# Smaller first transfers, bias copies one at a time, and weight blocks moved by 64 or 192 bytes

## The chip, the cores and the metric

One core of a Trainium2 chip runs the whole kernel as a single program. The metric is device time in microseconds (us), the median of repeated runs. A profile of one execution is shown beside it; "span" is the time from its first to its last instruction.

## The reference, cut to what matters

Two transformer blocks run one after the other on x of 512 rows by 1024 columns, all in float32. The first has a mixing layer of two kinds of attention, then cross attention to a memory of 256 rows, then an MLP; the second has windowed attention, a gated unit and another MLP.

```python
h = rms_norm(x, norm_mix[l])
proj = h @ w_in[l]
qa, ka, va, qg, kg, vg, glr, rg = jnp.split(proj, offsets, axis=-1)
o_a = moba_attention(qa, ka, va, rp_table)      # scores + a bias by distance, softmax, values
o_g = gla_chunked(qg, kg, vg, log_a)            # gated linear attention
x = x + concat(o_a, norm(o_g) * silu(rg)) @ w_out[l]
...                                             # cross attention, MLP, then the second block
```

The bias of a score depends on the head and on the distance between query and key alone.

## The kernel before

**Products.** All large matrix products are made of float32r matmuls of 128 rows by 128 weight columns by up to 512 moving columns. Each operand is split into a high part and a low part, so one product is three matmuls (`mm3`: high by high, high by low, low by high). `ah` and `al` hold the two parts of the normed activations, transposed, as 8 slices of 512 columns.

**Weights.** `weight_order` lists all weight units in the order of use. `load` (line 219) takes one unit: it allocates a block for the high part and one for the low part (`whi`, `wlo`, or one block `wu` for both where a unit has 1024 columns) from 10 slots of the tag `u8`, and then for each piece issues a DMA on SyncE's queue (SP) into one of three staging tiles `st` (line 233), an ACT copy that rounds to the high part (line 234) and a DVE subtraction for the low part (line 235). A unit of `w_in_u` is two pieces of 512 KB. `weight` (line 240) asks for the next unit and loads one unit ahead.

**Which operand is the weight block.** In `fm` the weight block is the stationary operand and `ah`/`al` move; in `tm` the activations are stationary and the weight block moves. Products with 256 moving columns are: `tm256` on units 2, 4, 7 and 9 of `w_in_u` (96 matmuls each), `mem_kv` on `w_xk` and `w_xv` (four units of 48 each), `fm_halves` on the first two units of `w_xq` and on units 2 and 3 of `w_in_2f` (96 each), `heads_v` on the two units of `w_in_2v` (96 each), and the first four units of `w_up` and of `w_up_2` (48 each). That is 384 + 384 + 384 + 192 + 384 = 1728 matmuls of the kernel's 8930 recorded ones. The first two units, `w_in_a`, are moved with 264 columns, so their slices of one k lie 1056 bytes apart.

**Places in SBUF.** A slot of `u8` has the size of its largest tile, 8 times 264 words, which is 8448 bytes or 33 times 256. In the built kernel `ah`, `al`, every `u8` block and the tiles of the phase pools start 192 bytes above a multiple of 256. `ident`, the moving operand of the transposes, starts 64 bytes lower in that count (128 above a multiple of 256): the tiles between it and `ah` are 512, 64, 512 and 2048 bytes, which is 12 times 256 and 64 more.

**Start.** `block1_mix` (line 404) loads the transposed x in four parts of two k slices (`x_piece`) between the three pieces of `w_in_a` unit 0 (rows k 0 to 2, 3 to 5, 6 to 7); only the first part comes in two transfers. Then the rows of x (`xin`) are loaded for the row sums.

**Bias of the attention scores.** `rel_bias` (line 540) makes a table `gd` of 8 heads by 640 distances in DRAM. `skew` (line 559) copies two heads of it to a DRAM tile `rd`, once for each of 128 rows (639 KB), so that a read with a shifted row length (`wbias`, line 569) gives the bias of two heads with the diagonal in place. There are four such copies: `rel_bias` calls `skew` once and each of the four `moba` calls calls it once more behind its own `wbias` load, until four are made. They depend on `gd` alone.

**Order.** The order of work is traced through small generator threads with hand-set delays; a planner of the framework then orders the instructions of each queue by that trace and by its own estimate of when each can start. Every engine and SP then works through its list in order: an instruction that waits holds up all that stand behind it on its engine. In the stretch that matters here the main thread runs, for each of two pairs: `pair` (line 514) for the linear attention's q and k, `pair` for the first attention pair's q and k, `moba` on these, `tm256` for v, another `pair` and `moba`, and `tm256` again.

Of the kernel before, what the change touches and what calls it, by code (L numbers as in the profile page):

```python
# [10 lines left out]
F32R = mybir.dt.float32r  # L11
# [9 lines left out]
P = 128  # L21
# [9 lines left out]
N_K2 = 19  # L31
N_M8 = 6
SCRATCH = 1024

PAD = 48
AHEAD = 1
# [6 lines left out]
def f32(ap):  # L43
    return ap.bitcast(F32)
# [65 lines left out]
class Kernel:  # L110
# [100 lines left out]
    def weight_ahead(self, n):  # L211
        while self.order and len(self.loaded) < n:
# [3 lines left out]
            else:  # L216
                self.loaded.append((o[:2], self.load(*o)))

    def load(self, key, idx, nk, w, after=None):

        nc = self.nc
        if nk * w == 1024:
            hl = self.u8([P, 2, nk, w], F32R, "wu")
            hi, lo = hl[:, 0], hl[:, 1]
        else:
            hi = self.u8([P, nk, w], F32R, "whi")
            lo = self.u8([P, nk, w], F32R, "wlo")
        src = self.I[key][idx].rearrange("p (a b) -> p a b", a=nk)
        step = 1024 // w
        for a in range(0, nk, step):  # L230
            s = slice(a, min(a + step, nk))
            st = self.sb.tile([P, s.stop - a, w], F32, tag="st", bufs=N_ST, name=self.name("st"))
            nc.sync.dma_start(st, src[:, s, :])
            nc.scalar.activation(hi[:, s, :], st, AF.Copy)  # L234
            nc.vector.tensor_sub(lo[:, s, :], st, f32(hi[:, s, :]))  # L235
            if after:
                after(a // step)
        return hi, lo

    def weight(self, *key, ahead=AHEAD):  # L240
# [163 lines left out]
    def block1_mix(self):  # L404
        nc, I, th = self.nc, self.I, self.th
        self.t_aux, self.t_tr = Tokens(2), Tokens(2)

        gm = self.sm([P, KT], "gmix")
        ex = [Event() for _ in range(KT)]

        def x_piece(j):
            st = self.k4([P, 2, T], F32, "xT")
            src = I["x_T"][j].rearrange("p (a t) -> p a t", a=2)
            if j:
                nc.sync.dma_start(st, src)
            for i in range(2):
                k = 2 * j + i
                if j == 0:
                    nc.sync.dma_start(st[:, i, :], src[:, i, :])
                if k == 0:  # L420
                    nc.sync.dma_start(gm, I["norm_mix"])
                if k == 1:
                    self.loaded.append((o[:2], self.load(*o, after=after)))
                nc.scalar.activation(self.ah[:, k, :], st[:, i, :], AF.Copy, scale=gm[:, k : k + 1])
                nc.vector.scalar_tensor_tensor(self.al[:, k, :], st[:, i, :], gm[:, k : k + 1], f32(self.ah[:, k, :]),
                                               op0=ALU.mult, op1=ALU.subtract)
                th.fire(ex[k])

        def after(i):
            if i < 2:  # L430
                x_piece(i + 1)
                if i == 1:
                    x_piece(3)

        o = self.order.pop(0)
        x_piece(0)
        self.weight_ahead(2)
        nc.sync.dma_start(self.ident, I["c_ident"])
        ss = self.sm([P, NC], "ssx")
        for c in range(NC):  # L440
            t = self.k4([P, D], F32, "xin")
            nc.sync.dma_start(t, I["x"][self.cs(c), :])
            nc.scalar.activation(self.junk, t, AF.Square, accum_out=ss[:, c : c + 1])
        rs = self.rstd(ss, NC, D)
        rsb = self.k2([P, T], F32, "rsb")

        va = self.u8([P, NC, 512], F32, "va")
        glr = self.k2([P, NC, 16], F32, "glr")
        w = self.weight("w_in_a", 0)
        ps = [self.acc() for _ in range(NC)]  # L450
        for k in range(KT):
            yield ex[k]
            for c in range(NC):
                self.mm3(ps[c][:, :264], *self.a_chunk(c)(k), w[0][:, k, :], w[1][:, k, :], k == 0, k == KT - 1)
        for c in range(NC):
            nc.scalar.activation(glr[:, c, :], ps[c][:, :16], AF.Copy, scale=rs[:, c : c + 1])
            nc.scalar.activation(va[:, c, 0:248], ps[c][:, 16:264], AF.Copy, scale=rs[:, c : c + 1])
        w = self.weight("w_in_a", 1)
        for c in range(NC):
            ps = (self.aux if c < 2 else self.tr)()  # L460
            self.tm(ps[:, :264], self.a_chunk(c), [w])
            nc.scalar.activation(va[:, c, 248:512], ps[:, :264], AF.Copy, scale=rs[:, c : c + 1])
        self.spread(rsb, rs, NC)
        self.rs, self.rsb = rs, rsb
        self.rel_bias()
        self.gla_consts(glr)
        yield 0.4
        oa = self.u8([P, NC, 512], F32, "oa")
        og = self.u8([P, 2, NC, 2, P], F32, "og")
        em = self.mem_norm()  # L470
        eo, eg = [Event() for _ in range(4)], [Event() for _ in range(2)]

        u = 0
        for pr in range(2):
            q, k, ev = yield from self.pair(u, 0.125)
            evr, vr = Event(), []
            th.spawn(self.gla(pr, q, k, ev, vr, evr, og[:, pr], eg[pr]), 2)
            q, k, ev = yield from self.pair(u + 1, -0.125)
            th.spawn(self.moba(2 * pr, q, k, ev, va, oa, eo[2 * pr]), 3)
            vr.append(self.k4([P, NC, 256], F32, "vg"))  # L480
            yield from self.tm256(u + 2, AF.Copy, vr[0])
            q, k, ev = yield from self.pair(u + 3, -0.125)
            th.spawn(self.moba(2 * pr + 1, q, k, ev, va, oa, eo[2 * pr + 1]), 3)
            vr.append(self.k4([P, NC, 256], F32, "rg"))
            yield from self.tm256(u + 4, AF.Silu, vr[1])
            th.fire(evr, 0.53)
            u += 5
        win = Event()
        th.fire(win)
        mix = [Event() for _ in range(NC)]  # L490

        def mix_T(c):
            yield eo + eg + [win]
            hi, lo = self.ah[:, :, self.cs(c)], self.al[:, :, self.cs(c)]
            self.split(oa[:, :, self.cs(c)], hi[:, 0:4, :], lo[:, 0:4, :])
            self.to_T(lambda k: og[:, k // 2, c, k % 2, :], 4, hi[:, 4:, :], lo[:, 4:, :])
            th.fire(mix[c], 2.29)

        for c in range(NC):
            th.spawn(mix_T(c), 1)  # L500
        yield from self.mem_kv(em)
        self.mix = mix
# [8 lines left out]
            self.mm(ps[:, self.cs(c)], self.ones, d, True, True)  # L511
        nc.scalar.activation(out, ps[:, : n * P], AF.Copy)

    def pair(self, u, sc):

        w = self.weight("w_in_u", u)
        ts = []
        for m in range(2):
            ps = self.acc()
            self.fm(ps, w, m, self.a_all())  # L520
            t = self.k2([P, T], F32, "qk")
            self.nc.vector.scalar_tensor_tensor(t, ps, sc if m == 0 else 1.0, self.rsb, op0=ALU.mult, op1=ALU.mult)
            ts.append(t)
            yield
        ev = Event()
        self.th.fire(ev, 1.12)
        return *ts, ev
# [31 lines left out]
    def skew(self):  # L559

        pr = len(self.rd)
        if pr < 4:
            self.rd.append(self.dp.tile([2, P * 639], F32, name=f"rd{pr}"))
            self.nc.sync.dma_start(self.rd[pr].rearrange("h (p l) -> p h l", l=639),
                                   self.gd[None, 2 * pr : 2 * pr + 2, :639].to_broadcast([P, 2, 639]))

    def moba(self, pr, q, k, ev, va, oa, done):
        nc, th = self.nc, self.th
        bias = self.k4([P, 2, 512], F32, "wbias")
        nc.sync.dma_start(  # L570
            bias, self.rd[pr][:, 127 : 127 + P * 638].rearrange("h (p l) -> p h l", l=638)[:, :, :512])
        self.skew()

        qd, ks = ([self.k2([P, T], F32R, n) for _ in range(2)] for n in ("qd", "ks"))
        ql = self.k2([P, T], F32R, "ql")
        for hh in range(2):
            o, x = slice(64 * hh, 64 * hh + 64), slice(64 - 64 * hh, 128 - 64 * hh)
# [1044 lines left out]
```

## Time and profile before

| | us |
|---|---|
| median of 3 runs | 1622.96 |
| lowest and highest of them | 1621.26, 1623.02 |
| time of the profiled execution | 1621.62 |
| span of its profile | 1619.8 |

The profile names engines PE (matmul), PEld (weight load), DVE, ACT, POOL and SP. Matmuls are pipelined, so the time that one matmul costs is read from the distance between the starts of one and the next, not from its own duration. PE is busy for 98% of the span, so a gain must come out of PE's own list: out of its gaps, its clock, or the distance from one matmul to the next.

### The profile page before, as it was taken

Reading aid. Unit: us, or ns where it says so; the run is one execution under the profiler, and the core shown is the slowest. Engines: PE = TensorE matmul, PEld = TensorE weight load, DVE = VectorE, ACT = ScalarE, POOL = GpSimd, SP = SyncE. Lnnn points to the kernel's source line nnn. Section 1 sums busy time; section 2 is a strip of 40 time slices with the busy share of each in tenths; the row PEclk is TensorE's granted clock in tenths of the full one; section 3 lists DMA queues with packets and bytes.
Section 4 is the critical chain, followed back from the end, with each engine's and each line's share of the span. In section 5 each row is a group of like instructions: output and inputs, shape, how many; then the busy total and the mean of one; then the engine's idle time right before and its main releaser. Section 6 shows DMA issues by size and latency. Waiting matters only on the chain.

```text
span 1619.8 us, 21884 instructions
## 1 busy us (share of the span) xinstructions
PE 1588.8 (98%) x8930; PEld 1350.9 (83%) x8930; DVE 971.9 (60%) x1194; ACT 686.3 (42%) x1052; POOL 530.8 (33%) x360
## 2 busy tenths in 40 slices
PE   9899999999999999999999999999999999999997
PEld 8777778898898888887799899888888988888876
DVE  4456475545565868686644554463345567686854
ACT  6446465333343535343423332374324435353431
POOL 0112220000016656573151441321011275656631
PEclk9899999999999999999999999999999999999999
DMA  8612133322142323214323203222424424232221
GB/s 293 182 41 92 44 115 104 139 84 78 64 159 78 132 89 119 89 65 156 98 72 130 91 14 105 105 78 79 150 97 156 169 79 143 78 130 78 82 101 65
DMA packets 50293, 171.08 MB, mean 106 GB/s; under 512 B 6192, under 2 KB 6720, under 8 KB 50192
## 3 DMA queue, kind: packets, MB, share of 16 engines
q1 hardware_dynamic: 50192, 169.68, 31.0%
q8 instruction: 70, 1.15, 0.3%
q14 instruction: 31, 0.25, 0.0%
HBM read 163.35 MB, written 8.93 MB: 106 GB/s over the span
## 4 chain that ended last, share of the span: by engine, by line
PE 44%; POOL 2%; DVE 2%; issue 1%; ACT 1%; DMA 0%; POOLq 0%; DVEq 0%; ACTq 0%
PE acc L290 34%; PE tr L290 7%; PE aux L290 2%; POOL raw L275 1%; PE tr L299 1%; DVE acc L1076 0%; DVE as L303 0%; DVE acc L1498 0%; DMA st<-in_w_down 0%; ACT junk L1486 0%; DVE wlo L235 0%; DVE wt L303 0%; POOL relu L1067 0%; DVE wu L235 0%; POOL relu L1025 0%
## 5 line engine op out<-in xcount | busy, mean ns | idle before, releaser
L290 PE MATMUL tr<-ah,wu 128*128 128x512 f32 x896 | 283.2, 389 | 0.0
L235 DVE TENSOR_TENSOR wlo<-st,whi 128x1024 fp32r<-128x1024 f32 (+1 forms) x158 | 200.6, 1296 | 130.4 <-ACT whi L234 104.2
L234 ACT ACTIVATE whi<-st 128x1024 fp32r<-128x1024 f32 (+1 forms) x158 | 160.4, 1044 | 204.2 <-PE acc L290 114.7
L290 PE MATMUL acc<-ah,whi 128*128 128x512 f32 (+1 forms) x576 | 213.2, 372 | 0.8 <-ACT ah L302 0.8
L290 PE MATMUL acc<-wt,as 128*128 128x512 f32 x864 | 206.3, 395 | 7.1 <-DVE acc L1076 3.7
L290 PE MATMUL acc<-al,whi 128*128 128x512 f32 (+1 forms) x576 | 212.1, 369 | 0.6 <-DVE al L303 0.6
L290 PE MATMUL acc<-ah,wlo 128*128 128x512 f32 (+1 forms) x576 | 211.7, 368 | 0.0
L303 DVE TENSOR_TENSOR wt<-raw,wt 128x1024 fp32r<-128x1024 f32 x84 | 169.9, 2037 | 55.4 <-ACT wt L302 47.6
L290 PEld LDWEIGHTS acc<-wt,as 128*128 128x128 f32 x864 | 164.8, 191 | 42.5 <-DVE acc L1076 4.2
L290 PEld LDWEIGHTS tr<-ah,wu 128*128 128x128 f32 x896 | 168.4, 188 | 34.9
L290 PE MATMUL tr<-al,wu 128*128 128x512 f32 x448 | 174.3, 389 | 0.0
L1025 POOL TENSOR_TENSOR relu<-relu 128x512 f32<-128x512 f32 x64 | 94.1, 1472 | 213.1 <-ACT relu L1024 186.3
L275 POOL TENSOR_TENSOR raw<-raw,raw 128x1024 f32<-128x1024 f32 x48 | 153.6, 3216 | 14.5 <-DMA raw<-in_w_down 9.6
L290 PE MATMUL acc<-whi,ah 128*128 128x512 f32 (+2 forms) x432 | 146.7, 347 | 1.2 <-ACT whi L234 1.2
L290 PE MATMUL acc<-wlo,ah 128*128 128x512 f32 (+2 forms) x432 | 147.6, 344 | 0.3 <-DVE wlo L235 0.3
L290 PE MATMUL acc<-whi,al 128*128 128x512 f32 (+2 forms) x432 | 147.4, 344 | 0.0
L302 ACT ACTIVATE wt<-raw 128x1024 fp32r<-128x1024 f32 x84 | 87.9, 1055 | 89.0 <-POOL raw L275 58.8
L290 PEld LDWEIGHTS acc<-ah,whi 128*128 128x128 f32 x576 | 108.7, 189 | 19.8 <-issue 1.7
L290 PEld LDWEIGHTS acc<-ah,wlo 128*128 128x128 f32 x576 | 109.0, 189 | 18.7 <-DVE wlo L235 0.9
L290 PEld LDWEIGHTS acc<-al,whi 128*128 128x128 f32 x576 | 109.2, 190 | 17.5 <-DVE al L303 0.8
L235 DVE TENSOR_TENSOR wu<-st,wu 128x1024 fp32r<-128x1024 f32 x64 | 107.8, 1691 | 25.6 <-ACT wu L234 25.6
L290 PEld LDWEIGHTS tr<-al,wu 128*128 128x128 f32 x448 | 84.3, 188 | 17.4
(344 smaller groups left out, 2815.3 us busy)
## 6 DMA issues: line engine op xcount, KB each, us to landing
st<-in_w_up SPq DMA_DIRECT2D x64, 512.0 KB, 3.7
raw<-in_w_down SPq DMA_DIRECT2D x48, 512.0 KB, 4.7
st<-in_w_in_2f SPq DMA_DIRECT2D x44, 512.0 KB, 4.4
st<-in_w_in_u SPq DMA_DIRECT2D x20, 512.0 KB, 4.7
st<-in_w_out SPq DMA_DIRECT2D x16, 512.0 KB, 4.4
st<-in_w_down SPq DMA_DIRECT2D x16, 512.0 KB, 4.5
st<-in_w_xk SPq DMA_DIRECT2D x8, 512.0 KB, 4.6
st<-in_w_xv SPq DMA_DIRECT2D x8, 512.0 KB, 4.1
```

The source lines that it names most:

```text
L234: nc.scalar.activation(hi[:, s, :], st, AF.Copy)
L235: nc.vector.tensor_sub(lo[:, s, :], st, f32(hi[:, s, :]))
L275: nc.gpsimd.tensor_sub(r[name][:, s, :], r[x][:, s, :], r[y][:, s, :])
L290: self.nc.tensor.matmul(ps, lhsT, rhs, start=start, stop=stop, skip_group_check=more)
L299: self.nc.tensor.transpose(ps, src, self.ident)
L302: self.nc.scalar.activation(hi, src, AF.Copy)
L303: self.nc.vector.tensor_sub(lo, src, f32(hi))
L1025: nc.gpsimd.tensor_mul(t, t, t)
```

## The change

It does three things.

1. The first weight unit is loaded in pieces of k rows 0, 1, 2 to 4, 5 to 7 (four pieces in place of three), ahead of everything else; the two single slices of x follow the first two pieces, two parts of x follow the third, and the last part the fourth. `norm_mix` follows the first slice of x.
2. `skew` is no longer called by `moba`. `rel_bias` makes the first copy; the other three are asked for inside `pair`, right behind the load of its weights, and each is tied on SP's queue behind the last weight transfer asked for until then (`issue_after(self.queued)`).
3. A `u8` block is now always 2112 words long, the size that the slot has anyway. The weights of units used in 256-column products start 16 words (64 bytes) into it where the block is stationary, and 48 words (192 bytes) where it moves. In both cases the stationary operand then starts 64 bytes (modulo 256) above the moving one; before, the two started on the same count.

No arithmetic changes, and the count of matmuls, splits and weight bytes is the same.

```diff
--- before.py
+++ after.py
@@ -31,6 +31,7 @@
 N_K2 = 19
 N_M8 = 6
 SCRATCH = 1024
+U8_WORDS = 2112
 
 PAD = 48
 AHEAD = 1
@@ -216,25 +217,38 @@
             else:
                 self.loaded.append((o[:2], self.load(*o)))
 
+    def offset(self, key, idx):
+
+
+        if key == "w_xk" or key == "w_xq" and idx < 2 or key == "w_in_2f" and idx in (2, 3) or key[:4] == "w_up" and idx < 4:
+            return 16
+        if key in ("w_xv", "w_in_2v") or key == "w_in_u" and idx % 5 in (2, 4):
+            return 48
+        return 0
+
     def load(self, key, idx, nk, w, after=None):
 
         nc = self.nc
+        off = self.offset(key, idx)
+        flat = lambda n: self.u8([P, U8_WORDS], F32R, n)[:, off : off + (2048 if w < 264 else nk * w)]
         if nk * w == 1024:
-            hl = self.u8([P, 2, nk, w], F32R, "wu")
+            hl = flat("wu").rearrange("p (s a n) -> p s a n", s=2, a=nk)
             hi, lo = hl[:, 0], hl[:, 1]
         else:
-            hi = self.u8([P, nk, w], F32R, "whi")
-            lo = self.u8([P, nk, w], F32R, "wlo")
+            hi, lo = (flat(n).rearrange("p (a n) -> p a n", a=nk) for n in ("whi", "wlo"))
         src = self.I[key][idx].rearrange("p (a b) -> p a b", a=nk)
         step = 1024 // w
-        for a in range(0, nk, step):
-            s = slice(a, min(a + step, nk))
+        cuts = (0, 1, 2, 5, 8) if after else range(0, nk + 1, step)
+        if cuts[-1] < nk:
+            cuts = (*cuts, nk)
+        for a, b in zip(cuts, cuts[1:]):
+            s = slice(a, b)
             st = self.sb.tile([P, s.stop - a, w], F32, tag="st", bufs=N_ST, name=self.name("st"))
-            nc.sync.dma_start(st, src[:, s, :])
+            self.queued = nc.sync.dma_start(st, src[:, s, :]).ins
             nc.scalar.activation(hi[:, s, :], st, AF.Copy)
             nc.vector.tensor_sub(lo[:, s, :], st, f32(hi[:, s, :]))
             if after:
-                after(a // step)
+                after(a)
         return hi, lo
 
     def weight(self, *key, ahead=AHEAD):
@@ -408,32 +422,24 @@
         gm = self.sm([P, KT], "gmix")
         ex = [Event() for _ in range(KT)]
 
-        def x_piece(j):
+        def x_piece(j, ks=(0, 1)):
             st = self.k4([P, 2, T], F32, "xT")
             src = I["x_T"][j].rearrange("p (a t) -> p a t", a=2)
-            if j:
-                nc.sync.dma_start(st, src)
-            for i in range(2):
+            s = slice(ks[0], ks[-1] + 1)
+            nc.sync.dma_start(st[:, s, :], src[:, s, :])
+            if (j, ks[0]) == (0, 0):
+                nc.sync.dma_start(gm, I["norm_mix"])
+            for i in ks:
                 k = 2 * j + i
-                if j == 0:
-                    nc.sync.dma_start(st[:, i, :], src[:, i, :])
-                if k == 0:
-                    nc.sync.dma_start(gm, I["norm_mix"])
-                if k == 1:
-                    self.loaded.append((o[:2], self.load(*o, after=after)))
                 nc.scalar.activation(self.ah[:, k, :], st[:, i, :], AF.Copy, scale=gm[:, k : k + 1])
                 nc.vector.scalar_tensor_tensor(self.al[:, k, :], st[:, i, :], gm[:, k : k + 1], f32(self.ah[:, k, :]),
                                                op0=ALU.mult, op1=ALU.subtract)
                 th.fire(ex[k])
 
-        def after(i):
-            if i < 2:
-                x_piece(i + 1)
-                if i == 1:
-                    x_piece(3)
-
+
+        after = {0: ((0, (0,)),), 1: ((0, (1,)),), 2: ((1,), (2,)), 5: ((3,),)}
         o = self.order.pop(0)
-        x_piece(0)
+        self.loaded.append((o[:2], self.load(*o, after=lambda a: [x_piece(*p) for p in after[a]])))
         self.weight_ahead(2)
         nc.sync.dma_start(self.ident, I["c_ident"])
         ss = self.sm([P, NC], "ssx")
@@ -475,11 +481,11 @@
             q, k, ev = yield from self.pair(u, 0.125)
             evr, vr = Event(), []
             th.spawn(self.gla(pr, q, k, ev, vr, evr, og[:, pr], eg[pr]), 2)
-            q, k, ev = yield from self.pair(u + 1, -0.125)
+            q, k, ev = yield from self.pair(u + 1, -0.125, pr > 0)
             th.spawn(self.moba(2 * pr, q, k, ev, va, oa, eo[2 * pr]), 3)
             vr.append(self.k4([P, NC, 256], F32, "vg"))
             yield from self.tm256(u + 2, AF.Copy, vr[0])
-            q, k, ev = yield from self.pair(u + 3, -0.125)
+            q, k, ev = yield from self.pair(u + 3, -0.125, True)
             th.spawn(self.moba(2 * pr + 1, q, k, ev, va, oa, eo[2 * pr + 1]), 3)
             vr.append(self.k4([P, NC, 256], F32, "rg"))
             yield from self.tm256(u + 4, AF.Silu, vr[1])
@@ -511,9 +517,11 @@
             self.mm(ps[:, self.cs(c)], self.ones, d, True, True)
         nc.scalar.activation(out, ps[:, : n * P], AF.Copy)
 
-    def pair(self, u, sc):
+    def pair(self, u, sc, skew=False):
 
         w = self.weight("w_in_u", u)
+        if skew:
+            self.skew()
         ts = []
         for m in range(2):
             ps = self.acc()
@@ -561,15 +569,16 @@
         pr = len(self.rd)
         if pr < 4:
             self.rd.append(self.dp.tile([2, P * 639], F32, name=f"rd{pr}"))
-            self.nc.sync.dma_start(self.rd[pr].rearrange("h (p l) -> p h l", l=639),
-                                   self.gd[None, 2 * pr : 2 * pr + 2, :639].to_broadcast([P, 2, 639]))
+
+            with self.tc.issue_after(self.queued) if pr else ExitStack():
+                self.nc.sync.dma_start(self.rd[pr].rearrange("h (p l) -> p h l", l=639),
+                                       self.gd[None, 2 * pr : 2 * pr + 2, :639].to_broadcast([P, 2, 639]))
 
     def moba(self, pr, q, k, ev, va, oa, done):
         nc, th = self.nc, self.th
         bias = self.k4([P, 2, 512], F32, "wbias")
         nc.sync.dma_start(
             bias, self.rd[pr][:, 127 : 127 + P * 638].rearrange("h (p l) -> p h l", l=638)[:, :, :512])
-        self.skew()
 
         qd, ks = ([self.k2([P, T], F32R, n) for _ in range(2)] for n in ("qd", "ks"))
         ql = self.k2([P, T], F32R, "ql")
```

## Rows read from the trace of the kernel before

**Rows 1.** The page, part 1: busy us, share of the span, instructions

```profile
PE 1588.8 (98%) x8930; PEld 1350.9 (83%) x8930; DVE 971.9 (60%) x1194; ACT 686.3 (42%) x1052; POOL 530.8 (33%) x360
```

**Rows 2.** PE's waits: us in total, times, longest; the longest of the list

```profile
PE aux L290 <- DVE ks L581: 4.9, 1, 4.9
```

**Rows 3.** Timeline of PE: start us, us, engine, line, operation, out<-in, shape, count

```profile
66.16 0.28 PE L290 MATMUL acc<-whi,al 128*128 128x256 f32 x1
71.35 0.44 PE L290 MATMUL aux<-ks,qd 128*128 128x128 f32 x1 [4.92 <-DVE ks L581]
...
73.79 0.48 PE L290 MATMUL aux<-ks,qd 128*128 128x128 f32 x1 [1.59 <-ACT qd L580]
...
75.09 0.58 PE L290 MATMUL acc<-whi,ah 128*128 128x256 f32 x1
...
80.38 0.41 PE L290 MATMUL aux<-ks,qd 128*128 128x256 f32 x1
...
81.78 0.50 PE L290 MATMUL acc<-ah,whi 128*128 128x512 f32 x1
```

**Rows 4.** Windows: busy us by engine (PE first), granted clock, DMA share, GB/s

```profile
70.78:81.02 10.24, 7.65 (x30) 6.83 (x30) 3.38 (x11) 5.83 (x15) 3.17 (x3) 0.50 0.00 0
```

**Rows 5.** Timeline of ACT, in brackets the idle time before and its releaser

```profile
61.32 1.06 ACT L234 ACTIVATE whi<-st 128x1024 fp32r<-128x1024 f32 x1 [11.54 <-DMA st<-in_w_in_u]
...
68.17 0.63 ACT L578 ACTIVATE ks<-qk 64x512 fp32r<-64x512 f32 x1 [2.60 <-DVE qk L522]
```

**Rows 6.** Timeline of SP's queue: DMAs issued

```profile
46.42 1.95 SPq L564 DMA_DIRECT2D rd<-gd  x3
48.48 0.81 SPq L233 DMA_DIRECT2D st<-in_w_in_u  x1
...
55.73 0.38 SPq L570 DMA_DIRECT2D wbias<-rd  x1
```

**Rows 7.** DMA from 44 to 64 us: all packets; issues, us to landing

```profile
DMA packets 1950, 5.30 MB, mean 265 GB/s; under 512 B 153, under 2 KB 153, under 8 KB 1947
...
rd<-gd SPq DMA_DIRECT2D x4, 639.0 KB, 13.0
```

**Rows 8.** Timeline of ACT, a later wait for a weight transfer

```profile
132.57 1.06 ACT L234 ACTIVATE whi<-st 128x1024 fp32r<-128x1024 f32 x1 [1.87 <-DMA st<-in_w_in_u]
```

**Rows 9.** Timeline of PE and of DVE in the first stage

```profile
7.48 0.74 PE L290 MATMUL acc<-whi,ah 128*128 128x264 f32 x4 [1.20 <-ACT whi L234]
...
27.25 0.71 DVE L235 TENSOR_TENSOR wlo<-st,whi 128x528 fp32r<-128x528 f32 x1 [3.62 <-ACT whi L234]
```

**Rows 10.** Timeline of PE: 24 matmuls of 256 columns lie between these two starts

```profile
60.04 0.28 PE L290 MATMUL acc<-whi,al 128*128 128x256 f32 x1
...
62.92 0.28 PE L290 MATMUL acc<-whi,al 128*128 128x256 f32 x1
```

**Rows 11.** Timeline of PE: the unit of 96 matmuls of 264 columns

```profile
19.81 0.41 PE L290 MATMUL aux<-whi,ah 128*128 128x264 f32 x2
...
28.59 0.40 PE L290 MATMUL aux<-whi,ah 128*128 128x264 f32 x2
...
31.55 0.39 PE L290 MATMUL acc<-ah,whi 128*128 128x512 f32 x1
```

**Rows 12.** PE: 24 matmuls of 512; 26 with stationary columns 16 bytes apart

```profile
40.05 0.39 PE L290 MATMUL acc<-ah,whi 128*128 128x512 f32 x1
...
45.49 0.39 PE L290 MATMUL acc<-ah,whi 128*128 128x512 f32 x1
...
863.17 0.40 PE L290 MATMUL acc<-wlo,ah 128*128 128x512 f32 x1
...
869.28 0.39 PE L290 MATMUL acc<-whi,ah 128*128 128x512 f32 x1
```

**Rows 13.** Timeline of PE: four transposes between these two starts

```profile
336.67 0.60 PE L299 MATMUL tr<-ident,xn 128*128 128x128 f32 x4
337.11 0.27 PE L299 MATMUL aux<-ident,xn 128*128 128x128 f32 x1
```

## The prediction, made before the run

> **What bounds the kernel now.** I read the page's busy times first: PE is busy for 98% of the span, DVE for 60%, ACT for 42% [rows 1]. The kernel is its list of matmuls, so the change can gain only in three places: where PE stands still, where its clock is low, and in the distance from one matmul to the next. PE's waits come second. The longest is a single one of 4.9 us on DVE's `ks` [rows 2], and PE's timeline puts it at 66 to 71 us [rows 3]. The windows show what it drags along: from 70.78 to 81.02 the granted clock is 0.50, the lower level of 1.2 GHz, behind an idle stretch of 5 us [rows 4]. Third, I followed that wait back. ACT makes `ks` at 68.17, and in its in-order list stands, before that, a weight copy `whi` that waited 11.54 us for its transfer and ran at 61.32 [rows 5]. SP explains the transfer: three bias copies `rd` went out at 46.42, just ahead of it at 48.48 [rows 6], a fourth is close behind, and each of the four (639 KB) took a median of 13.0 us to land while all packets together moved at 265 GB/s [rows 7]. Only the first `rd` is wanted soon. So a queue filled with copies that nobody needs yet delays a weight that nobody needs yet, and ACT's order turns that into a stop of PE. Last I took the distance between matmul starts: 256 columns take 2.88/24 = 120.0 ns [rows 10], 512 take 5.44/24 = 226.7 ns [rows 12].
>
> **The bias copies one by one.** What the stop costs: the last matmul before it starts at 66.16 and takes 0.12, so PE stands from 66.28 to 71.35, 5.07 us [rows 3, 10]. The four matmuls of 71.35 to 75.09 take 3.74 [rows 3]; four of twice the columns take 1.40 at the end of the same stretch (80.38 to 81.78), so 0.7 to 1.4 is due and 2.3 to 3.0 is lost, 2.7 taken. The 24 matmuls from 75.09 to 80.38 take 5.29 where 24 take 2.88 at full clock: 2.4 [rows 3, 10]. The last four lose some 0.3, less than half of their 1.40 because the clock returns by 81.02 [rows 3, 4]. Sum 10.5 us.
>
> How much of it goes: a copy's share of the DMA is 639/265 = 2.4 us [rows 7]. Three copies less ahead of or beside the weight's transfer bring it 3 times 2.4 = 7.2 us forward, the low bound. With one copy ahead SP issues it at about 47.1 (1.95 us was for three issues [rows 6]), and 639 + 512 KB at 265 GB/s take 4.3 us: 51.4 in place of 61.3, 9.9 us forward, the high bound. I take the middle, 8.5. PE would ask for the first of the four matmuls at 66.28 instead of 71.35 and for the last of them near 67.1 instead of 74.7, so 7.6 us forward ends the stop. At 8.5 there are 0.9 us to spare; at the low bound 0.4 stays. So the whole 10.5 goes, 10.1 at the low bound. What is late next is then no operand but PE itself. The `wbias` read (55.73 [rows 6]) still goes behind its own `rd`, which lands earlier than now.
>
> What the moved copies cost: each now stands behind a weight transfer on SP, and everything behind it on SP stands behind its 2.4 us of DMA. The copy behind unit 4's load falls into a stretch in which the next weight has time. The one behind unit 7's load falls near 129 us, and there ACT already waits 1.87 us for a transfer at 132.57 [rows 8]. From 0 to 2.4 us could be added to that wait; PE sees it only if ACT's later work is late, as it was above. I take 0.5, near the low end, because today's 1.87 has no wait of PE of its size beside it. The last one is behind unit 9's load, and the next weight copy is far off: nothing.
>
> **The first transfers.** A first piece of one k row and one slice of x let PE start before 7.48, where its first matmul waits 1.20 for `whi` [rows 9]. But the stage ends when the last rows have come: DVE finishes the low part of rows 6 and 7 at 27.25 + 0.71 = 27.96, and PE takes them at 28.59 [rows 9, 11], 0.63 later. An earlier start therefore buys 0 to 0.63 us. Against that stands one transfer more in the queue: an issue takes 0.38 to 0.81 us of SP [rows 6], and a landing that moves by more than 0.63 becomes PE's. Bounds -0.6 and +0.8; I take -0.3, as the bytes are the same and the spare covers most of an issue.
>
> **The offsets.** They touch 384 + 384 + 384 + 192 + 384 = 1728 matmuls, so 1 ns is 1.73 us. 226.7 - 120.0 = 106.7 ns is what 256 columns take; a fixed 13.3 ns is left at either width [rows 10, 12]. The question is whether that comes from both operands starting on the same count modulo 256. The nearest row that tells is the 264-column unit, where that relation moves on by 32 bytes with each k: 264 columns take 110.0 by themselves, and the 72 matmuls of k 0 to 5 take 8.78/72 = 121.9, the 24 of k 6 and 7 2.96/24 = 123.3 [rows 11]. So relations other than 0 leave a fixed part of 11.9 to 13.3, and the new one (moving operand 192 ahead, modulo 256, which is k 6) is within the dearer pair. The farther row is the transposes, with the new relation but of full float32: (337.11 - 336.67)/4 = 110.0 [rows 13], only 3.3 above 106.7. And a stationary operand whose columns lie 16 bytes apart costs 6.11/26 = 235.0, 8.3 above 226.7 [rows 12]. So the bounds are -10.0 and +8.3 ns. I take -1.5, near the 264-column unit (0 to -1.4), which is the same kind of matmul: -2.6 us. ACT and DVE write the blocks at other places too; with 42% and 60% busy [rows 1] that is nothing.
>
> The relation of starts is thus seen to matter by 1.4 ns at most in the nearest rows. The Trainium skill (TensorE: Matmul & The Clock Gate, section Step-by-step: what each phase is for) speaks against this part of the change: it says that the streaming operand and the weight load have a read port each, so that loading doesn't take bandwidth from the running matmul. By that rule the offset is worth nothing and the sum is 1611.3; the 8.3 ns of the strided weights [rows 12] show that the stationary's layout does reach the spacing here, so the rule isn't the whole story.
>
> **Sum.** -10.5 + 0.5 - 0.3 - 2.6 = -12.9. The profiled run took 1621.62, against a median of 1622.96 and a span of 1619.8, so 1608.7, in round numbers 1609; against the median it would be 1610.
>
> **The rivals.**
> *Nothing from the offset.* -10.5 + 0.5 - 0.3 gives 1611.3. For it: k 6 and 7 at 123.3, exactly 8 columns over 120.0 [rows 11]. It differs from the forecast by the spacing alone.
> *The offset takes most of the fixed part.* Spacing near 110, as in the transposes [rows 13]: 10.0 times 1728 = 17.3, and -10.3 - 17.3 gives 1594. Against it stands the 264-column unit. In the Trainium skill (same page, section Back-to-back issue gap) the gap of warm matmuls taken singly is the columns at 2.4 GHz plus 2.5 ns, 109.2 for 256, an estimate which would give -18.7; the rows here show 120.0.
> *The stop is only moved.* ACT waits at another landing, as at 132.57 [rows 8], or the tied copy delays the weight after it: half of the 10.5 stays. 1621.6 - 5.3 + 0.2 = 1616.5.
> *The change doesn't do what it says.* The planner orders SP by its own estimate and may still put the copies together, and the offset is nothing: 1621.6.
> *Slower: the new relation is dear.* The stationary operand, starting elsewhere, costs what the strided one does: 8.3 times 1728 = +14.3, and 1621.6 - 10.3 + 14.3 = 1625.6. It decides from 6.0 ns on (10.3/1.728); by the nearest rows the effect is at most 0.
>
> **How the numbers follow.** Forecast 0.32 (1609); nothing from the offset 0.15 (1611.3); most of the fixed part 0.25 (1594); stop moved 0.15 (1616.5); not done 0.07 (1621.6); slower 0.06 (1625.6). The range leaves out the last two, 0.13: its upper end is 1617, and its lower end 1591 is the third case with the first transfers and the copies at their good ends and a spacing of 109. 0.2% is 3.2 us, about what a measurement of this kernel can tell from no change. Faster by more than that: the first four, 0.87; within it 0.07; slower 0.06.
>
> **What would show it.** After: ACT has no wait of 11 us, SP shows the four `rd` apart, PE has no gap near 66 us and no window at 0.50 from 70 to 81. If the window stays, the stop is moved. 24 matmuls of 256 columns over their starts give the offset: near 118.5 is the forecast, 120 the first rival, 110 the second, above 126 the slower one. The first matmul starts earlier, while the rows of k 6 and 7 are taken no more than 0.6 us earlier. Near 129 to 135 us ACT's wait tells what the moved copy cost. The prediction is wrong if PE waits for a weight that was on time before, or if the spacing falls well below 118.

## The result and the profile after

| | before | after |
|---|---|---|
| median of 5 runs, us | 1622.96 | 1610.89 |
| lowest and highest, us | 1619.33, 1624.02 | 1610.17, 1616.09 |
| span of the profile, us | 1619.8 | 1609.1 |

The ratio is 0.9934, with a 95% interval from 0.9919 to 0.9949: 8.3 to 13.1 us less. 1609 was predicted, between 1591 and 1617. The time came out as forecast, the parts of it did not.

The page's first part for the kernel after (busy us, share of the span, instructions, by engine) answers to [rows 1]. PE is still the bound, and is busy for 8.6 us less:

```profile
PE 1580.2 (98%) x8930; PEld 1342.8 (83%) x8930; DVE 971.2 (60%) x1195; ACT 686.6 (43%) x1053; POOL 531.0 (33%) x360
```

PE's list of waits (us in total, times, longest) answers to [rows 2]. The 4.9 us on `ks` is down to 0.8; the wait on `qd` behind it, 1.59 before [rows 3], is 1.9:

```profile
PE aux L304 <- ACT qd L589: 1.9, 1, 1.9
...
PE aux L304 <- DVE ks L590: 0.8, 1, 0.8
```

PE's timeline at the place of the old stop, and the window of its half clock, answer to [rows 3] and [rows 4]. The four matmuls now wait 0.76, 1.86 and 0.57 us, 3.2 in all, and 3.4 us run at 0.50 in place of 10.2:

```profile
66.29 0.30 PE L304 MATMUL aux<-ks,qd 128*128 128x128 f32 x1 [0.76 <-DVE ks L590]
...
68.70 0.33 PE L304 MATMUL aux<-ks,qd 128*128 128x128 f32 x1 [1.86 <-ACT qd L589]
69.60 0.47 PE L304 MATMUL aux<-ks,ql 64*128 64x128 f32 x1 [0.57 <-POOL ql L591]
```

```profile
69.46:72.88 3.42, 3.28 (x14) 3.16 (x15) 1.49 (x8) 1.75 (x7) 0.88 (x2) 0.50 0.00 0
```

So the stop has shrunk, not gone. The reason is seen on ACT, whose timeline answers to [rows 5]:

```profile
52.32 1.06 ACT L248 ACTIVATE whi<-st 128x1024 fp32r<-128x1024 f32 x1 [4.64 <-DMA st<-in_w_in_u]
53.56 1.06 ACT L248 ACTIVATE whi<-st 128x1024 fp32r<-128x1024 f32 x1 [0.19 <-DMA st<-in_w_in_u]
57.18 0.69 ACT L697 ACTIVATE lse<-aux,bgate 128x512 f32<-128x512 f32 x1 [2.55 <-DVE bcum L696]
...
63.08 0.64 ACT L587 ACTIVATE ks<-qk 64x512 fp32r<-64x512 f32 x1 [2.60 <-DVE qk L530]
```

The last weight copy ahead of `lse` ran at 61.32 and now runs at 53.56, as its transfer lands: 7.8 us earlier, within the 7.2 to 9.9 that was worked out. But `ks`, the step that PE needs, moved from 68.17 to 63.08, only 5.1. Between them stands `lse` at 57.18, and it now waits for DVE's `bcum`. DVE's timeline after, and below it the same `bcum` before:

```profile
53.41 2.47 DVE L249 TENSOR_TENSOR wlo<-st,whi 128x1024 fp32r<-128x1024 f32 x2 [3.88 <-ACT whi L248]
55.80 0.68 DVE L530 SCALAR_TENSOR_TENSOR qk<-acc,rsb 128x512 f32<-128x512 f32 x1
56.40 0.74 DVE L696 TENSOR_SCALAR bcum<-aux,bgate 128x512 f32<-128x512 f32 x1
```

```profile
52.19 0.75 DVE L687 TENSOR_SCALAR bcum<-aux,bgate 128x512 f32<-128x512 f32 x1 [0.36 <-PE aux L290]
```

Before, DVE had made `bcum` at 52.19, long before ACT was free; now it does two weight subtractions (2.47 us, 53.41) and a `qk` first. SP shows why they come together, and answers to [rows 6]:

```profile
43.88 0.64 SPq L574 DMA_DIRECT2D rd<-gd  x1
44.63 2.42 SPq L247 DMA_DIRECT2D st<-in_w_in_u  x2
...
51.27 0.55 SPq L574 DMA_DIRECT2D rd<-gd  x1
```

The transfers of unit 4 are now both behind `rd` (two `st` at 44.63), where one had been ahead of the four copies. One `rd` is ahead of them, as the change says, the next follows at 51.27. The later wait on ACT answers to [rows 8] and is the same, 2.00 against 1.87 us, so the copy that was moved there adds 0.13 us on ACT and nothing that PE shows:

```profile
125.99 1.06 ACT L248 ACTIVATE whi<-st 128x1024 fp32r<-128x1024 f32 x1 [2.00 <-DMA st<-in_w_in_u]
```

The first matmul answers to [rows 9], 5.42 against 7.48:

```profile
5.42 0.37 PE L304 MATMUL acc<-whi,ah 128*128 128x264 f32 x1
```

The spacing answers to [rows 10]. Two pairs of PE rows, 24 matmuls of 256 columns between the rows of each pair:

```profile
57.01 0.28 PE L304 MATMUL acc<-wlo,ah 128*128 128x256 f32 x1
...
59.84 0.28 PE L304 MATMUL acc<-wlo,ah 128*128 128x256 f32 x1
...
457.43 0.28 PE L304 MATMUL acc<-al,wu 128*128 128x256 f32 x1
...
460.15 0.28 PE L304 MATMUL acc<-al,wu 128*128 128x256 f32 x1
```

2.83/24 = 117.9 ns in unit 2 of `w_in_u`, 2.72/24 = 113.3 ns in the first units of `w_up`, against 120.0. There are 72 stretches of 24. Over starts that follow each other without a gap the mean of the 72 fell from 119.6 to 116.0 ns: 28 stretches are at 117.6 to 118.0, 19 at 114.0 or below, the others mix the two. 3.6 ns times 1728 is 6.2 us.

How the gain grows along PE's list, from the starts in both traces of the matmul that has n others before it:

| n | before, us | after, us | gain, us |
|---|---|---|---|
| 300 | 50.03 | 49.27 | 0.76 |
| 400 | 66.04 | 65.14 | 0.90 |
| 500 | 93.14 | 86.70 | 6.44 |
| 1000 | 130.42 | 123.61 | 6.81 |
| 3000 | 392.92 | 383.85 | 9.07 |
| 8000 | 1394.06 | 1382.32 | 11.74 |
| last | 1610.28 | 1599.42 | 10.86 |

0.76 from the first transfers, 5.5 from the stop (400 to 500), 5.3 from there to 8000, nearly all of it spacing, and 0.9 given back near the end, where a wait of PE on DVE's `acc` is 4.80 us in place of 3.74.

### The profile page after: what moved, and what is told of

It reads as the page before. It is cut to its first block, busy times and chain, and to the rows that moved or that the text cites. A ratio compares the mean times of both kernels' runs of the same rounds, so it can differ in the third digit from the quotient of the medians.

```text
span 1609.1 us, 21890 instructions
## 1 busy us (share of the span) xinstructions
PE 1580.2 (98%) x8930; PEld 1342.8 (83%) x8930; DVE 971.2 (60%) x1195; ACT 686.6 (43%) x1053; POOL 531.0 (33%) x360
## 4 chain that ended last, share of the span: by engine, by line
PE 44%; POOL 2%; DVE 2%; issue 1%; ACT 1%; DMA 0%; POOLq 0%; DVEq 0%; ACTq 0%
PE acc L304 34%; PE tr L304 7%; PE aux L304 2%; POOL raw L289 1%; PE tr L313 1%; DVE acc L1085 0%; DMA st<-in_w_down 0%; DVE as L317 0%; DVE acc L1507 0%; ACT junk L1495 0%; DVE wlo L249 0%; DVE wt L317 0%; POOL relu L1076 0%; DVE wu L249 0%; POOL relu L1034 0%
## 5 line engine op out<-in xcount | busy, mean ns | idle before, releaser
L249 DVE TENSOR_TENSOR wlo<-st,whi 128x1024 fp32r<-128x1024 f32 (+3 forms) x159 | 200.6, 1286 | 125.0 <-ACT whi L248 100.2
L248 ACT ACTIVATE whi<-st 128x1024 fp32r<-128x1024 f32 (+3 forms) x159 | 160.9, 1039 | 196.9 <-PE acc L304 113.2
```

## The experiments

**One part at a time.** Three kernels, each the kernel before with one part of the diff, all beside the same runs of before (median 1622.95). The first, the smaller first transfers:

```diff
+        cuts = (0, 1, 2, 5, 8) if after else range(0, nk + 1, step)
...
+        after = {0: ((0, (0,)),), 1: ((0, (1,)),), 2: ((1,), (2,)), 5: ((3,),)}
```

> The kernel before with the first part of the change alone (smaller first transfers). From the two traces: the stage behind it begins 0.7 us earlier, so 0.7 us off the time, about 1622.2 beside 1622.96, within the noise of 3.2 us. If the stage is held by the last rows of the first two units, as the prediction had it, 0 to 0.6. A rival, that the earlier start is what lets the later copies land earlier, would show as several us here.

Measured: 1621.78, ratio 0.999 (0.9979 to 1.0001), between 3.4 us less and 0.2 more. Its 300th matmul starts 1.0 us earlier, and by the 500th 0.2 is left. The 0 to 0.7 us that were expected fit, and the time can't tell them from nothing. PE's stop is still there:

```profile
70.09 0.45 PE L293 MATMUL aux<-ks,qd 128*128 128x128 f32 x1 [4.67 <-ACT ks L573]
```

In this kernel SP issues the four copies two and two, one pair ahead of each piece of unit 4 (43.85 and 45.84 us), not three and one as in [rows 6], so the copies didn't stay quite as they were. `ks` comes late all the same, 10.2 us at half clock follow, and an earlier PE mostly waits longer.

The second, the bias copies alone:

```diff
+            with self.tc.issue_after(self.queued) if pr else ExitStack():
...
-        self.skew()
```

> The kernel before with the second part alone (bias copies one by one). By the trace of the changed kernel the landing of unit 4's weights comes 9 us earlier, but two ACT copies and two DVE subtractions now stand ahead of the gate's chain, which comes only 5.1 us earlier: a gain of 5.5 us, about 1617.5, with waits of PE near 66 to 70 us of 0.8 and 1.9 us and one half-clock stretch of 3.4 us there. By the prediction's own step (the whole stop goes) 10.0 to 10.5 us, about 1612.5.

Measured: 1618.05, ratio 0.9967 (0.9954 to 0.998), 3.2 to 7.5 us less. The 10 us of the prediction are excluded. ACT's timeline of this kernel has the order of the kernel after, a weight copy that waits and then a `lse` that waits for `bcum`:

```profile
55.78 1.06 ACT L234 ACTIVATE whi<-st 128x1024 fp32r<-128x1024 f32 x1 [4.90 <-DMA st<-in_w_in_u]
59.39 0.69 ACT L691 ACTIVATE lse<-aux,bgate 128x512 f32<-128x512 f32 x1 [2.55 <-DVE bcum L690]
```

The copy ran 5.54 us earlier than before (61.32), and `ks` 2.89 earlier (65.28 in place of 68.17): some 2.6 us are lost between the two, as in the kernel after (7.8 and 5.1). The 500th matmul starts 5.64 us earlier, although the start of this execution was late; the first matmul waits longer than in [rows 9]:

```profile
8.91 1.01 PE L290 MATMUL acc<-whi,ah 128*128 128x264 f32 x4 [2.68 <-ACT whi L234]
```

The third, the offsets alone:

```diff
+        flat = lambda n: self.u8([P, U8_WORDS], F32R, n)[:, off : off + (2048 if w < 264 else nk * w)]
```

> The kernel before with the third part alone (weight blocks 64 or 192 bytes further on). By the spacing in the changed kernel's trace (some 116 in place of 119.5 ns, 1728 matmuls) a gain of 5.5 to 6.5 us, about 1617, and the same two spacings, 117.8 and 113.3, in stretches of 24 matmuls. By the prediction 2.6 us, 1620.4, at 118.5 ns. If the spacing fell for another reason (an order of instructions that the other parts changed), it stays at 120 here and the time does not move.

Measured: 1614.87, ratio 0.9948 (0.9932 to 0.9965), 5.7 to 11.0 us less. The mean spacing of the 72 stretches is 116.0, and nearly every stretch has the value that it has in the kernel after. So the offset is the cause of the shorter spacing, and it is worth 6.2 us by its spacing. The middle of the interval, 8.4, is above that; in the profiled execution 3.2 us were gained before the 500th matmul, where the stop was shorter because the weight's copy ran at 59.38 in place of 61.32 and only 3.4 us ran at half clock behind it. The first matmul was late here too, 8.66, waiting 2.88 for `whi`.

The three ratios add up to some 15 us, the whole change gives 8.3 to 13.1. The sum of the three has an uncertainty of about 4 us, so this is no contradiction.

**Is it the order on ACT?** The kernel before with its four copies left as they were, and unit 4's split queued behind the gate's chain:

```diff
+            with ExitStack() as es:
+                if (key, idx) == ("w_in_u", 4):
+                    for i in self.gate:
+                        es.enter_context(self.tc.issue_after(i))
+                nc.scalar.activation(hi[:, s, :], st, AF.Copy)
+                nc.vector.tensor_sub(lo[:, s, :], st, f32(hi[:, s, :]))
...
+        i1 = nc.scalar.activation(e, e, AF.Ln, bias=1.0)
...
+        i2 = nc.vector.tensor_tensor_scan(b, self.rst, e, 0.0, op0=ALU.mult, op1=ALU.add)
+        self.gate = (i1.ins, i2.ins)
```

> The kernel before, with its four copies together as they were, but with ACT's two copies and DVE's two subtractions of unit 4 queued behind the gate's scan. If the stop is only the order of ACT's list (a weight copy that waits stands ahead of the gate's chain), PE's 4.9 us wait on ks and the 10.2 us at half clock go although the landing is as late as before: a gain of 9.5 to 10.5 us, about 1613. If the copies hurt by themselves (what PE waits for is late through DMA, or the bias read wbias is), half or more of the stop stays: 1617 or above.

Measured: 1616.21, ratio 0.9956 (0.9942 to 0.9971). ACT and PE of this kernel:

```profile
56.16 0.69 ACT L692 ACTIVATE lse<-aux,bgate 128x512 f32<-128x512 f32 x1 [7.82 <-DVE bcum L691]
...
59.36 1.05 ACT L238 ACTIVATE whi<-st 128x1024 fp32r<-128x1024 f32 x1
61.83 1.06 ACT L238 ACTIVATE whi<-st 128x1024 fp32r<-128x1024 f32 x1 [1.42 <-DMA st<-in_w_in_u]
```

```profile
69.47 0.22 PE L294 MATMUL aux<-ks,qd 128*128 128x128 f32 x1
...
70.41 0.33 PE L294 MATMUL aux<-ks,qd 128*128 128x128 f32 x1 [0.15 <-ACT qd L584]
```

The weight still comes late (61.83, with a wait of 1.42), but `lse` is ahead of it, and of PE's stop 0.15 us is left; no stretch at half clock follows. The 400th matmul starts 3.19 us later than before, the 500th 6.79 earlier: 9.98 us for the whole stop, as its parts had been summed. (The late start doesn't flatter this: the gate's chain begins with a matmul, and so came later with PE.) So the stop is a matter of ACT's order, and the bias copies did harm only through it. The time fell by 4.7 to 9.4 us, a little short of the 9.5 that was expected. The profiled execution is the slowest of the six (1620.19), and in it the rest gave part of the gain back: 3.2 us were lost at the start (first matmul at 8.41, waiting 2.91 for `whi`, and 6.8 us at half clock), and another 4.2 by the 2000th matmul, where stretches at half clock near 141, 189 and 223 us last 17.1 us in all, against 6.8 before. What the other five lost isn't on record.

The same edit on the kernel after:

> The changed kernel, with ACT's two copies and DVE's two subtractions of unit 4 queued behind the gate's scan. In the changed kernel PE still waits 0.8, 1.9 and 0.6 us near 66 to 70 us and 3.4 us run at half clock (1.7 us lost): 5 us of the stop are left. If the gate's chain is what is late there, because it stands behind two copies and two subtractions, all of it goes: 1610.9 - 5 = 1606. If the landing of the bias or another chain is what is late next, less than 2 us go: 1609 or above.

Measured: 1608.23, ratio to before 0.9906 (0.989 to 0.9921), between the two values expected. The four matmuls run through, and the 500th starts 4.57 us earlier than in the kernel after:

```profile
65.67 0.22 PE L308 MATMUL aux<-ks,qd 128*128 128x128 f32 x1
...
66.32 0.33 PE L308 MATMUL aux<-ks,qd 128*128 128x128 f32 x1
```

So the rest of the stop was the gate's chain too, and there is no further chain behind it. In this execution all of the 4.57 was given back by the 2000th matmul. The windows show where: the granted clock between 125 and 240 us, here and then in the kernel after (the figure after POOL's):

```profile
125.00:160.00 35.00, 35.00 (x190) 26.48 (x190) 20.41 (x53) 20.52 (x39) 4.08 (x4) 0.90 0.33 106
160.00:200.00 40.00, 40.00 (x320) 31.95 (x319) 20.24 (x49) 16.86 (x40) 9.24 (x9) 0.96 0.26 92
200.00:240.00 40.00, 37.98 (x483) 30.84 (x482) 29.28 (x67) 25.66 (x50) 11.81 (x8) 0.91 0.20 69
```

```profile
125.00:160.00 35.00, 35.00 (x213) 26.28 (x212) 22.27 (x58) 19.91 (x38) 5.66 (x5) 0.95 0.44 146
160.00:200.00 40.00, 40.00 (x335) 31.93 (x333) 19.52 (x47) 18.15 (x43) 9.24 (x9) 1.00 0.25 84
200.00:240.00 40.00, 37.98 (x495) 31.08 (x494) 30.36 (x71) 26.48 (x52) 11.99 (x8) 0.96 0.23 77
```

0.90, 0.96 and 0.91 against 0.95, 1.00 and 0.96: 17.1 us at half clock here, 6.8 there, and half of the 10.2 more is 5.1. PE's list is the same in both but for 15 places near the old stop; why its clock fell more here was not settled. By its median this kernel is the fastest of all, but its interval overlaps that of the kernel after.

**Which distance, and for which width?** The kernel after with other distances for the 256-column products, the stationary operand 128, 192, 96 and 32 bytes above the moving one (modulo 256). In `offset`, for the stationary and for the moving case:

```diff
-            return 16
+            return 32    # 128; 48 for 192, 24 for 96, 8 for 32
...
-            return 48
+            return 32    # 128; 16 for 192, 40 for 96, 56 for 32
```

> The changed kernel with the stationary operand 128 bytes above the moving one (32 words in both kinds of product) in place of 64. If any start other than the same one will do, spacing stays at 113 to 118 ns and the time at 1611. If 64 is special, or if 128 is as dear as the 264-column unit has it (123.7 ns there at 128, 122.2 at 64, 121.1 at 0), spacing is back at 120 ns or above: 1617 to 1620.

> The changed kernel with the stationary operand 64 bytes below the moving one (192 modulo 256). If any start other than the same one will do, spacing 113 to 118 ns and 1611. If the stationary operand has to start behind the moving one, 120 ns and 1617.

> The changed kernel with the stationary operand of the 256-column products 96 bytes above the moving one in place of 64. Between 64 (113.3 or 117.8 ns) and 128 (118.6): if the spacing follows the distance smoothly, 116 to 118.6 ns, 1611 to 1616. If there are steps with a good window that 64 only touches, the better of the two values throughout, 113.3 ns, and a gain of 4 to 5 us on the changed kernel: 1606.

> As the run before, at 32 bytes. Between 0 (120.0 ns) and 64: smoothly 117 to 119 ns, 1612 to 1617; with the good window of which 64 is the upper end, 113.3 ns and 1606.

PE rows, 24 matmuls of the first units of `w_up` between each two, in the order 128, 192, 96, 32:

```profile
459.43 0.28 PE L304 MATMUL acc<-al,wu 128*128 128x256 f32 x1
...
462.28 0.28 PE L304 MATMUL acc<-al,wu 128*128 128x256 f32 x1
```

```profile
460.98 0.28 PE L304 MATMUL acc<-al,wu 128*128 128x256 f32 x1
...
463.81 0.28 PE L304 MATMUL acc<-al,wu 128*128 128x256 f32 x1
```

```profile
463.32 0.28 PE L304 MATMUL acc<-al,wu 128*128 128x256 f32 x1
...
466.13 0.28 PE L304 MATMUL acc<-al,wu 128*128 128x256 f32 x1
```

```profile
461.58 0.28 PE L304 MATMUL acc<-al,wu 128*128 128x256 f32 x1
...
464.42 0.28 PE L304 MATMUL acc<-al,wu 128*128 128x256 f32 x1
```

| distance, bytes | these 24, ns | mean of the stretches, ns | median, us | ratio to before |
|---|---|---|---|---|
| 0 (before) | 120.0 | 119.6 | 1622.96 | 1 |
| 32 | 118.3 | 118.3 | 1615.63 | 0.9953 (0.9937 to 0.9969) |
| 64 (after) | 113.3 | 116.0 | 1610.89 | 0.9934 (0.9919 to 0.9949) |
| 96 | 117.1 | 117.9 | 1613.08 | 0.9942 (0.9919 to 0.9965) |
| 128 | 118.8 | 118.8 | 1614.92 | 0.9954 (0.9939 to 0.9969) |
| 192 | 117.9 | 117.7 | 1614.74 | 0.9948 (0.9932 to 0.9963) |

Each ratio is to the runs of before made beside that kernel. By the spacing any distance beats none, and 64 is the best of those tried. The times alone can't show either: all rows but the first hold the other two parts of the change as well, no kernel with these and distance 0 was run, and the intervals of the last five rows overlap. It is the distance that counts and not the block's own place: a block that starts 16 words in goes at 113.3 in part of the stretches where it is stationary (distance 64), and at 117.8 in nearly every one where it moves (distance 192).

Neither the smooth course nor the window of steps that had been expected fits: 113.3 is there at 64 alone, and at 64 only in part of the stretches. What selects between 113.3 and 117.8 stays open. The same stretches have the same value in the kernel after and with the offsets alone, so it isn't chance alone; but the distance doesn't fix it. The kernel after and the same with the tie place their blocks alike, and the same 24 matmuls of a unit of `w_in_2f` (256 columns) go at different paces in the two:

```profile
805.32 0.28 PE L304 MATMUL acc<-ah,wlo 128*128 128x256 f32 x1
...
808.04 0.28 PE L304 MATMUL acc<-ah,whi 128*128 128x256 f32 x1
```

```profile
806.19 0.28 PE L308 MATMUL acc<-ah,wlo 128*128 128x256 f32 x1
...
809.02 0.28 PE L308 MATMUL acc<-ah,whi 128*128 128x256 f32 x1
```

2.72/24 = 113.3 and 2.83/24 = 117.9 ns. In both a stretch at half clock ends shortly before, at 803.3 and at 805.2 us, at another matmul of the list. So the pace of a stretch depends on what went before it; by what, these runs don't show.

Then the products of 512 columns, which had been left at 0 (226.7 ns, [rows 12]); the kernel at 64 has the same places as this diff, written another way:

```diff
+        if key in ("w_xq", "w_in_2f", "w_branch_a_2", "w_branch_b_2") or key[:4] == "w_up" or key == "w_in_u":
+            return 16    # 64; 32 for 128, 48 for 192
+        return 0 if key == "w_in_a" else 48    # 64; 32 for 128, 16 for 192
```

> The changed kernel with the same 64-byte relation for the weight blocks of 512-column products too (4128 matmuls more by the loops of the code). If the fixed 13.3 ns of a 512-column matmul gives way as that of a 256-column one did (2.2 or 6.7 ns), the time falls by 9 to 28 us, 1583 to 1602, and 24 matmuls of 512 columns take 5.28 to 5.39 in place of 5.44 us. If the shorter distance is a matter of 256 columns alone, spacing stays at 226.7 ns and the time at 1611.

> The changed kernel with the stationary operand of the 512-column products of weight units 128 bytes above the moving one (4128 matmuls; they stand at 0 in the changed kernel and cost 226.7 ns, and at 64 they cost 233.3). Theory: the distance of the two starts decides at which point of a running matmul the reading of the next weights meets it, so each width has its own good and bad distances, in steps of some 6.7 ns. Then 128 gives 220, 226.7 or 233.3 ns: a change of -27, 0 or +27 us on 1611. Rival: for 512 columns any distance but 0 is bad: 233.3 and 1638.

> As the run before, at 192 bytes. By the first theory 220, 226.7 or 233.3 ns again, not needed to be that of 128; by the rival 233.3 ns and 1638 us.

PE rows at 64, 128 and 192, 24 matmuls of 512 columns between the first and the second of each:

```profile
546.21 0.40 PE L304 MATMUL tr<-ah,wu 128*128 128x512 f32 x1
...
551.81 1.55 PE L304 MATMUL acc<-wt,as 128*128 128x512 f32 x6
```

```profile
528.47 0.40 PE L306 MATMUL tr<-ah,wu 128*128 128x512 f32 x1
...
534.06 2.21 PE L306 MATMUL acc<-wt,as 128*128 128x512 f32 x9
```

```profile
530.61 0.39 PE L306 MATMUL tr<-ah,wu 128*128 128x512 f32 x1
...
536.11 2.20 PE L306 MATMUL acc<-wt,as 128*128 128x512 f32 x9
```

5.60/24 = 233.3, 5.59/24 = 232.9 and 5.50/24 = 229.2 ns. Over all 512-column matmuls on weight units that follow each other without a gap (some 3970) the means are 227.4 at 0 and 233.5, 233.0 and 229.7. The times are 1631.1 (ratio 1.0044, 1.0027 to 1.006), 1628.09 (1.0043, 1.0022 to 1.0064) and 1619.48 (0.9975, 0.9959 to 0.999), all slower than the kernel after. The rule of "64 above" turns into a loss of 6.6 ns a matmul at the other width: for 512 columns the same start is the best of the four, as the rival had it, though 192 costs less than it said. The theory of steps of 6.7 ns isn't borne out: 229.2 is on none of them, and no run shows what happens inside a matmul. Moving the 512-column blocks also changed 256-column products of which nothing had moved: with the 512-column blocks at 64 the second and third 24 of unit 2 of `w_in_u` went at 113.3 in place of 117.8, and the last three 24 of `w_up_2` at 117.8 in place of 113.3.

## Why the prediction was right, and where it was not

The time was right because two terms were wrong in opposite directions: 5.0 us too much for the copies, 3.6 too little for the offsets. That they nearly cancel is luck. By the prediction's own signs, the window at 0.50 that stayed (69.46 to 72.88) says that the stop was in part moved, and a spacing well below 118 in part of the stretches that the offset was sized wrong.

*The bias copies: -10.5 predicted, -5.5 in the trace.* The terms of the stop were right: with the order changed alone, 9.98 us went. The transfer's 8.5 us were nearly right too, 7.8 measured. The step that failed is the sentence that takes the 8.5 us from the weight's landing to PE undiminished. It held ACT's and DVE's lists to be as they had been; in the new order both subtractions of unit 4 stand ahead of `bcum`, which had been ready before, and `lse` waits 2.55 us for it. 7.8 at the landing is 5.1 at `ks`, and by the prediction's own need of 7.6 that leaves 2.5 us of stop; 3.2 and 1.7 of half clock were left. The rival "the stop is only moved" had the size right, half of the stop; but its mechanism, another landing or a weight behind the tied copy, is not what happened: ACT's wait is for `bcum`.

*The moved copies: +0.5 predicted, 0 measured*, within the bounds of 0 to 2.4: 2.00 against 1.87 us on ACT, and the gain of PE goes on from 6.81 to 7.09 across it.

*The first transfers: -0.3 predicted, -0.8 in the two traces*, a little past the bound of -0.6. The step held between these two traces: a first matmul 2.06 us earlier left 0.64 by the 100th matmul and 0.76 by the 300th, about the 0.63 us of spare that was read, all of it and not half. By itself the part was worth 0.2 us at the 500th matmul, behind the stop, and nothing that the time shows. What the prediction had no row for is that the old first transfers are often late: with them the first matmul started at 7.48 in the kernel before, and at 8.91, 8.66 and 8.41 in three kernels of the experiments, each with half clock beside it; in the ten kernels with the smaller ones it started between 5.06 and 6.16, and no stretch at half clock came before 67 us. The profile of before that the sum stood on was one of the good starts.

*The offsets: -2.6 predicted, -6.2 by the spacing.* The term was mis-sized: -1.5 ns was taken, -3.6 came, between the bounds of -10.0 and +8.3. The row that was taken as nearest, the unit of 264 columns ([rows 11]), misled. Its two groups differ by 1.4 ns, but each mixes several distances, so they don't set 64 against 0; and the runs show that a good distance at one width isn't one at another. The far row, the transposes ([rows 13]), erred to the other side.

The Trainium skill's rule (TensorE: Matmul & The Clock Gate, section Step-by-step: what each phase is for), that streaming and weight loading have a read port each, was read in the prediction as making the offset worth nothing. The traces differ from that reading: 120.0 ns at 0 and 113.3 at 64 for 256 columns, 226.7 and 233.3 for 512, with no other edit. The measurement decides; where the two operands start does reach the spacing. Why it does, no run shows.

## What to carry to other kernels

A transfer that comes earlier is worth what arrives at the engine that waits: read the in-order lists between the two again in the new order, or tie the copy that nobody needs yet behind the chain that somebody does. Where a stop stands behind it, an earlier start is worth nothing until the stop is gone. Measure an offset between two operands at the width that it is for, and over many stretches: one stretch can take either of two paces.

## What the runs showed of the hardware

The distance between the starts of a matmul's two operands moves the spacing of float32r matmuls by up to 7 ns either way: for 256 columns 120.0 at 0 and 113.3 or 117.8 at 64 bytes, for 512 columns 226.7 at 0 and 233.3, 232.9 and 229.2 at 64, 128 and 192. At 64 bytes the same 24 matmuls, placed alike, went at 113.3 in one kernel and 117.9 in another. Half-clock time up to the last matmul differs between profiles by more than the change's smaller terms: 27.3 us in the kernel before, 20.5 after, 34.1 and 27.3 in the two kernels with the tie. Some half of each is lost. In those two profiles a gain of 10.0 and of 4.6 us at one place was in part and wholly given back by the 2000th matmul.
